# Low parts, complex differences and rotation products of the Hyena and attention layers: from GpSimd and VectorE in turn to VectorE alone

## The chip, the cores and the metric

The kernel runs on one core of one Trainium2 chip. The metric is the device time of one execution in microseconds (us); the median of several runs is compared. Engines are named as in the profile: PE is TensorE (PEld its weight load), DVE is VectorE, ACT is ScalarE, POOL is GpSimd, SP is SyncE, which issues nearly all loads.

## The reference, cut to what matters

Two stacks of two layers work on 256 tokens of width 1024. The first stack is untouched by the change. The second is a Hyena layer and an attention layer, each followed by a mixture of 16 experts:

```python
for i in range(DEPTH):
    u = rms_norm_2(h, mix_norm_g[i])
    if i % N_MIXERS == 0:
        proj = u @ hy_w_in[j]                       # 1024 x 2560
        main_in, cq = proj[..., :3 * D_MAIN], proj[..., 3 * D_MAIN:]
        main = hyena_mixer(main_in, hy_short_w[j], k_fft, hy_skip[j])
    else:
        proj = u @ at_w_in[j]                       # 1024 x 1536
        ...
        q = apply_axial_rope(rms_norm_2(q, at_q_norm_g[j]), cos, sin)
        kk = apply_axial_rope(rms_norm_2(kk, at_k_norm_g[j]), cos, sin)
        main = blocked_gqa(q, kk, vv)
    cross = memory_cross_attn(cq, mem_n, w_mem_kv[i])
    h = h + jnp.concatenate([main, cross], axis=-1) @ w_out[i]
    h = h + expert_choice_ffn(rms_norm_2(h, ffn_norm_g[i]), router_w[i], ...)
```

`hyena_mixer` is a short filter of three taps, then twice a long convolution by Fourier transform, `irfft(rfft(z) * k)`, and a gate.

## The kernel before, in words

Everything is float32. A product of two float32 matrices is made of three matmuls: each operand is split into a high part (a rounded copy) and a low part (what the rounding left out), and `mm3` (L303 to L305) adds high times high, high times low and low times high. `split` (L283) makes the parts of a weight tile: ACT writes the high part `hi` (L290), and then `next(lo_engines[0])` (L291), POOL and DVE in turn, writes the low part `lo` as a subtraction. In the output projection both parts lie in one tile `hl`. There are three `hi` and three `lo` buffers, so the fourth split waits until PE has used the first. A weight unit of the input projection is a 128x1024 tile, and 24 matmuls use it.

The Hyena layer (`hyena_layer`) computes the input projection as units of a pipeline (`dense_T`, tiles `psT`); `short` (L1324 to L1331) takes each result from PSUM, scales it by the row norm `nR` and applies the three taps into `uv` and `ux`, which PE then transposes (L1349). `nR` comes from a chain of small DVE instructions (L359, L360, L311 to L322, L365), a matmul by the identity (`psr`, L370) and a copy (L372). Four tasks `chain(o, n)`, for two orders and two halves of the channels, transform (`psz`), multiply by the filter in complex numbers (four products `ya`, L1368 to L1371, a difference, L1372, and a sum, L1373), split the result into `yh` and `yl` (L1376, L1377), transform back (`psy`), gate, and in the second order split the gated result into `ah` and `al` (L1397, L1398). `out_second` is the output projection (`psO`).

The attention layer (`attention_layer`) projects, scales (`qk_done`), and rotates (`rotate`): each query and key is multiplied by a cosine table (L1465) and its swapped halves by a sine table (L1463, into `rot`). Attention of pairs of heads follows (`attend`), with the softmax on DVE and ACT, and the same output projection.

Each of the two layers ends with the router (`route`) and the experts, whose weights (1.5 MB loads) stream through a ring of SBUF slots; a slot is loaded again when its last reader is done. Instructions of one engine run in the order of the program, which the framework's scheduler sets from the code; an instruction that waits holds all behind it on its engine. The engines on which low parts are made are in three lists:

```python
lo_engines = [cycle((G, V))]
LO1 = (G, V)
LO2 = (V, G, V)
LO3 = (G, V)
```

`LO1` holds from the start of the Hyena layer, `LO2` from that of the attention layer and `LO3` in its output projection.

Of the kernel before, what the change touches and what calls it, by code (L numbers as in the profile page):

```python
# [12 lines left out]
F32 = mybir.dt.float32  # L13
# [5 lines left out]
ALU = mybir.AluOpType  # L19
# [180 lines left out]
def build(ctx, tc, I, C, out, upto="all", dbg=None):  # L200
# [75 lines left out]
        S.activation(junk[:, :1], after, AF.Exp, scale=0.0)  # L276

    lo_engines = [cycle((G, V))]
    LO1 = (G, V)
    LO2 = (V, G, V)  # L280
    LO3 = (G, V)

    def split(src, shape, together=False):  # L283
        if together:
# [1021 lines left out]
    def hyena_layer(hy, ring, nm, c2, kd, kvd, state):  # L1306
        lo_engines[0] = cycle(LO1)
        state["go"] = True
        sw = c2["sw"]
        sk = cols[:, at["hy_skip_2"]:at["hy_skip_2"] + 12]  # L1310
        w_in = rows_of(I["hy_w_in_2"][0])
        u = {n: hy.tile([128, 6, T], F32, name=f"u{n}") for n in ("v", "x1", "x2")}
        cqT = hy.tile([128, 2, T], F32, name="cqT")
        kv = memory_load(hy, kvd)
        ready, box, busy = set(), {}, []
        has = lambda n, bs: (lambda: all((n, b) in ready for b in bs))

        def proj(n, c0, **kw):

            def short(b0, ps):  # L1320
                while nm.R is None:
                    pipe.tick()
                tmp = hy.tile([128, 2, T], F32, tag="tmp", name="tmp")
                V.tensor_tensor(tmp, ps, nm.R[:, None, :].to_broadcast([128, 2, T]), op=ALU.mult)  # L1324
                for q in range(2):
                    b = b0 + q
                    cb = c0 // 128 + b
                    o = u[n][:, b]
                    S.activation(o, tmp[:, q], AF.Copy, scale=sw[:, 18 + cb:19 + cb])
                    V.scalar_tensor_tensor(o[:, 1:], tmp[:, q, :T - 1], sw[:, cb:cb + 1], o[:, 1:], op0=ALU.mult, op1=ALU.add)  # L1330
                    V.scalar_tensor_tensor(o[:, :T - 1], tmp[:, q, 1:], sw[:, 36 + cb:37 + cb], o[:, :T - 1], op0=ALU.mult, op1=ALU.add)  # L1331
                    ready.add((n, b))

            return dense_T(ring, w_in[:, :, c0:c0 + 768], nm.xh, nm.xl, short, **kw)

        def chain(o, n):

            bs = range(3 * n, 3 * n + 3)
            c = slice(384 * n, 384 * n + 384)
            z = u["x1" if o else "v"]  # L1340
            yield from wait(has("z" if o else "v", bs))
            kf = hy.tile([128, 4, 384], F32, tag="uv" if o and n else "kf", name="kf")
            nc.sync.dma_start(kf, kd[2 * o + n])
            zz = hy.tile([128, 2, 2, 384], F32R, tag="z", name="zz")
            zh, zl = zz[:, 0], zz[:, 1]
            for par in range(2):
                ps = B("pst", [128, 384])
                for j in range(3):
                    PE.transpose(ps[:, 128 * j:128 * j + 128], z[:, 3 * n + j, par::2], ident)  # L1349
                S.activation(zh[:, par], ps, AF.Copy)  # L1350
                V.tensor_tensor(zl[:, par], ps, zh[:, par].bitcast(F32), op=ALU.subtract)
            yield from wait(lambda: "F" in box)
            Fh, Fl, Vh, Vl = box["F"]
            yield from wait(lambda: len(busy) < 1)
            busy.append((o, n))
            yh = hy.tile([128, 4, 384], F32R, tag="yh", name="yh")
            yl = hy.tile([128, 4, 384], F32R, tag="yl", name="yl")
            yield
            for f in range(2):
                pz = []  # L1360
                for part in range(2):
                    ps = B("psz", [128, 384])
                    fc = slice(part * 256 + f * 128, part * 256 + f * 128 + 128)
                    for t in range(2):
                        mm3(ps, Fh[:, t, fc], Fl[:, t, fc], zh[:, t], zl[:, t], t == 0, t == 1)
                    pz.append(ps)
                a = [hy.tile([128, 384], F32, tag="ya", name="ya") for _ in range(4)]
                V.tensor_tensor(a[0], pz[0], kf[:, f], op=ALU.mult)  # L1368
                V.tensor_tensor(a[1], pz[1], kf[:, 2 + f], op=ALU.mult)
                V.tensor_tensor(a[2], pz[0], kf[:, 2 + f], op=ALU.mult)  # L1370
                V.tensor_tensor(a[3], pz[1], kf[:, f], op=ALU.mult)  # L1371
                G.tensor_tensor(a[0], a[0], a[1], op=ALU.subtract)  # L1372
                V.tensor_tensor(a[2], a[2], a[3], op=ALU.add)  # L1373
                for part in range(2):
                    b = 2 * part + f
                    S.activation(yh[:, b], a[2 * part], AF.Copy)  # L1376
                    (G if part and not o else V).tensor_tensor(yl[:, b], a[2 * part], yh[:, b].bitcast(F32), op=ALU.subtract)  # L1377
                yield
            gate = u["x2" if o else "x1"]
            yield from wait(has("x2" if o else "x1", bs))  # L1380
            if o:
                yield from wait(lambda: "a" in box)
            yield
            for cb in range(3):
                b = 3 * n + cb
                i = 6 * o + b
                sz = hy.tile([128, T], F32, tag="sz", name="sz")
                S.activation(sz, z[:, b], AF.Copy, scale=sk[:, i:i + 1])
                ps = B("psy", [128, T])
                cc = slice(128 * cb, 128 * cb + 128)  # L1390
                for f in range(4):
                    mm3(ps, yh[:, f, cc], yl[:, f, cc], Vh[:, f], Vl[:, f], f == 0, f == 3)
                V.scalar_tensor_tensor(sz, ps, rn[:, i:i + 1], sz, op0=ALU.mult, op1=ALU.add)
                if o:
                    ah, al = box["a"]
                    V.tensor_tensor(sz, sz, gate[:, b], op=ALU.mult)
                    S.activation(ah[:, b], sz, AF.Copy)  # L1397
                    (V if n else G).tensor_tensor(al[:, b], sz, ah[:, b].bitcast(F32), op=ALU.subtract)  # L1398
                    ready.add(("a", b))
                else:  # L1400
                    V.tensor_tensor(gate[:, b], sz, gate[:, b], op=ALU.mult)
                    ready.add(("z", b))
                yield
            busy.remove((o, n))

        for o in range(2):
            for n in range(2):
                pipe.spawn(chain(o, n))
        pipe.feed(proj("v", 1536, need=lambda i: nm.halves > i, k_major=True))
        F = []  # L1410
        for name in ("fwd", "inv"):
            raw = ring.one(C[name])
            hi = hy.tile(list(raw.shape), F32R, name=name + "h")
            lo = hy.tile(list(raw.shape), F32R, name=name + "l")
            S.activation(hi, raw, AF.Copy)
            V.tensor_tensor(lo, raw, hi.bitcast(F32), op=ALU.subtract)
            F += [hi, lo]
        box["F"] = F
        pipe.feed(proj("x1", 0))
        wq = ring.one(w_in[:, :, 2304:2560])  # L1420

        def cq_done(j, ps):
            V.tensor_tensor(cqT, ps, nm.R[:, None, :].to_broadcast([128, 2, T]), op=ALU.mult)
            ready.add("cq")

        ct = pipe.spawn(cross_task(kv, cqT, hy, lambda: "cq" in ready, lambda: box.get("a"), (V, S)))
        pipe.feed(dense_T(ring, None, nm.xh, nm.xl, cq_done, tiles=[wq[:, 0:4], wq[:, 4:8]]))
        pipe.feed(proj("x2", 768))
        pipe.flush()
        box["a"] = ah, al = [xtp.tile([128, 8, T], F32R, tag=f"x{s}", name=f"a{s}") for s in "hl"]  # L1430
        pipe.feed(out_second(ring, I["w_out_2"][0], ah, al, state, lambda k: ct[1] if k > 5 else ("a", k) in ready))
        pipe.flush()

    def attention_layer(late, pool, ring, nm, c2, kvd, state, wqk):
# [17 lines left out]
        def rotate(i):  # L1452
# [7 lines left out]
            for t in range(2):  # L1460
                for j, a, nh in ((1, 768, 4), (0, 512, 4)) if i else ((0, 0, 8),):
                    for g in range(2):
                        G.tensor_tensor(hx(rot[:, t, a:a + 64 * nh])[:, :, :, g], hx(qk[:, t, a:a + 64 * nh])[:, :, :, 1 - g],  # L1463
                                        xhf(tg[:, j, t, 1])[:, None, :, g].to_broadcast([128, nh, 2, 16]), op=ALU.mult)
                    V.tensor_tensor(hv(qk[:, t, a:a + 64 * nh]), hv(qk[:, t, a:a + 64 * nh]), tg[:, j, t, 0][:, None, :].to_broadcast([128, nh, 64]), op=ALU.mult)  # L1465
            s2 = ss.rearrange("p t h -> p (t h)")
# [523 lines left out]
    o, ss = fin  # L1990
# [31 lines left out]
```

## Time and profile before

| what | value |
|---|---|
| median of 3 runs | 1913.12 us (1909.66 to 1913.76) |
| profiled execution | 1915.09 us, of which 1913.3 us are the span from the first to the last instruction |
| PE busy | 1643.7 us, 86% of the span |
| DVE busy | 981.1 us, 51% |
| ACT busy | 665.7 us, 35% |
| POOL busy | 540.2 us, 28%, 330 instructions |
| read from HBM | 483.41 MB |

The busy share is a mean over stages with different limits. Times below are from the start of the span: the Hyena layer lies at about 976 to 1127, the experts behind it end at 1450, the attention layer reaches to 1567, and the second experts run to the end.

### The profile page before, as it was taken

The numbers are of one execution on the slowest core, as the hardware profiler recorded it, in microseconds if no ns is written. First come the engines' busy times: TensorE is split into PE (matmuls) and PEld (weight loads), VectorE is DVE, ScalarE is ACT, GpSimd is POOL, SyncE is SP. The second block draws the span as 40 slices with busy tenths as digits, with TensorE's granted clock in tenths as the row PEclk, the third lists the DMA queues.
The fourth block names the chain that finished last, engine by engine and source line by source line (L and its number), as shares of the span: only waits on it lengthen the run. The fifth ranks groups of instructions, "written<-read, shape, count | busy, mean of one in ns | idle before, by whom it ended". The sixth has DMA issues, their size and how long they took to land. (4 is left out here: it accounts for less than half of the span.)

```text
span 1913.3 us, 27291 instructions
## 1 busy us (share of the span) xinstructions
PE 1643.7 (86%) x11139; PEld 1201.3 (63%) x11139; DVE 981.1 (51%) x1642; ACT 665.7 (35%) x1100; POOL 540.2 (28%) x330
## 2 busy tenths in 40 slices
PE   8899988999998999999989989676667999766665
PEld 7898977788988979899978765222224655211221
DVE  7987467666489865754568763010104873100102
ACT  4346444454443464545444432000003552000000
POOL 4532455754445325444434220000002220000001
PEclk9999999999999999999999989898988999898987
DMA  6443554455633435755443679999999768999997
GB/s 237 128 133 123 179 181 157 162 194 170 211 125 102 161 124 174 259 196 182 152 160 121 221 285 420 425 425 425 425 413 335 265 247 362 425 426 424 426 420 254
DMA packets 136516, 490.42 MB, mean 256 GB/s; under 512 B 11152, under 2 KB 32067, under 8 KB 115911
## 3 DMA queue, kind: packets, MB, share of 16 engines
q1 hardware_dynamic: 135919, 488.11, 67.8%
q8 instruction: 87, 1.43, 0.3%
q10 hardware_dynamic: 472, 0.57, 0.1%
q14 instruction: 38, 0.31, 0.0%
HBM read 483.41 MB, written 5.24 MB: 255 GB/s over the span
## 5 line engine op out<-in xcount | busy, mean ns | idle before, releaser
L291 POOL TENSOR_TENSOR lo<-w,hi 128x1024 fp32r<-128x1024 f32 (+3 forms) x163 | 379.1, 2327 | 806.5 <-ACT hi L290 776.4
L290 ACT ACTIVATE hi<-w 128x1024 fp32r<-128x1024 f32 (+3 forms) x330 | 327.3, 997 | 347.7 <-PE psT L305 178.9
L304 PE MATMUL psT<-xh,lo 128*128 128x256 f32 x1328 | 382.1, 288 | 12.4 <-POOL lo L291 12.4
L303 PE MATMUL psT<-xh,hi 128*128 128x256 f32 x1328 | 388.6, 293 | 2.0 <-ACT hi L290 2.0
L305 PE MATMUL psT<-xl,hi 128*128 128x256 f32 x1328 | 381.6, 287 | 0.0
L291 DVE TENSOR_TENSOR lo<-w,hi 128x1024 fp32r<-128x1024 f32 (+3 forms) x167 | 223.2, 1337 | 145.4 <-ACT hi L290 144.7
L304 PEld LDWEIGHTS psT<-xh,lo 128*128 128x128 f32 x1328 | 259.5, 195 | 18.1 <-POOL lo L291 14.2
L303 PEld LDWEIGHTS psT<-xh,hi 128*128 128x128 f32 x1328 | 259.2, 195 | 10.1 <-issue 5.9
L305 PEld LDWEIGHTS psT<-xl,hi 128*128 128x128 f32 x1328 | 259.3, 195 | 1.8 <-issue 1.8
L1738 PE MATMUL psx<-w,late 128*32 128x256 f32 (+1 forms) x1024 | 155.3, 539 | 75.8 <-DMA w<-in_exp_w_up 40.5
L1738 PEld LDWEIGHTS psx<-w,late 128*32 128x32 f32 x1024 | 47.0, 115 | 181.5 <-issue 74.2
L1738 PE MATMUL psx<-w,xg 128*32 128x256 f32 (+1 forms) x1024 | 124.1, 538 | 36.6 <-DMA w<-in_exp_w_up 19.9
L1790 PE MATMUL psy<-w,late 128*32 128x512 f32 x576 | 95.3, 596 | 38.2 <-DMA w<-in_exp_w_down 34.3
L1774 ACT ACTIVATE yy<-psy,rslot 128x512 fp32r<-128x512 f32 (+1 forms) x17 | 11.3, 662 | 320.7 <-PE psy L1790 249.7
L1738 PEld LDWEIGHTS psx<-w,xg 128*32 128x32 f32 x1024 | 39.9, 116 | 117.5 <-issue 60.6
L305 PE MATMUL acc<-lo,hh 128*128 128x512 f32 x256 | 100.7, 393 | 1.9 <-POOL lo L291 1.9
L304 PE MATMUL acc<-hi,hlo 128*128 128x512 f32 x256 | 100.8, 394 | 0.0
L303 PE MATMUL acc<-hi,hh 128*128 128x512 f32 x256 | 100.5, 393 | 0.0
L1982 POOL TENSOR_TENSOR o<-X,gf 128x256 f32<-128x256 f32 (+1 forms) x6 | 6.1, 1042 | 326.5 <-DVE X L1780 326.5
L1775 DVE SCALAR_TENSOR_TENSOR yy<-psy,rslot,yy 128x512 fp32r<-128x512 f32 (+1 forms) x17 | 12.2, 719 | 163.4 <-ACT yy L1774 162.9
L1754 DVE TENSOR_TENSOR late<-late,psx 128x512 f32<-128x512 f32 (+1 forms) x16 | 8.1, 550 | 166.8 <-PE psx L1738 166.8
L1790 PEld LDWEIGHTS psy<-w,late 128*32 128x32 f32 x576 | 26.6, 109 | 102.6 <-DMA w<-in_exp_w_down 52.4
(494 smaller groups left out, 2945.3 us busy)
## 6 DMA issues: line engine op xcount, KB each, us to landing
w<-in_exp_w_gate SPq DMA_DIRECT2D x64, 1536.0 KB, 27.8
w<-in_exp_w_up SPq DMA_DIRECT2D x64, 1536.0 KB, 29.5
w<-in_exp_w_down SPq DMA_DIRECT2D x48, 1536.0 KB, 28.5
w<-in_w_in SPq DMA_DIRECT2D x39, 1024.0 KB, 5.1
w<-in_w_up SPq DMA_DIRECT2D x32, 1024.0 KB, 5.7
w<-in_w_down SPq DMA_DIRECT2D x32, 1024.0 KB, 6.8
w<-in_exp_w_down SPq DMA_DIRECT2D x18, 1024.0 KB, 14.3
w<-in_w_out SPq DMA_DIRECT2D x10, 1024.0 KB, 5.6
```

The costliest lines, as they stand in the source:

```text
L290: S.activation(hi, src, AF.Copy)
L291: next(lo_engines[0]).tensor_tensor(lo, src, hi.bitcast(F32), op=ALU.subtract)
L303: PE.matmul(ps, lh, rh, start=start, stop=False)
L304: PE.matmul(ps, ll, rh, start=False, stop=False)
L305: PE.matmul(ps, lh, rl, start=False, stop=stop)
L1738: mm = PE.matmul(pg[nm][n][32 * e:32 * e + 32, :c1 - c0], xg[gr // 2][:, k, 128 * (gr % 2) + 32 * e:128 * (gr % 2) + 32 * e + 32], wt[e][: ...
L1754: V.tensor_tensor(hid[:, c], sg[:, :n], pg["up"][i][:, :n], op=ALU.mult)
L1774: S.activation(yh, py, AF.Copy, scale=rs[:, 2, gr:gr + 1])
L1775: V.scalar_tensor_tensor(yl, py, rs[:, 2, gr:gr + 1], yh.bitcast(F32), op0=ALU.mult, op1=ALU.subtract)
L1790: PE.matmul(py[n][32 * e:32 * e + 32], hT[:, k, 32 * e:32 * e + 32], wt[e][:, k - k0, 512 * n:512 * n + 512], start=k == 0, stop=k == 5, t ...
L1982: G.tensor_tensor(o[:, t, c], X[:, t, c], gf[:, c], op=ALU.mult)
```

## The change

All low parts of the two layers, the complex difference (L1372), all `yl` and `al`, and the sine products of the rotation are issued on DVE. POOL keeps the memsets, the small tables of the router and part of the router's row copies. The first stack keeps its two engines. The code:

```diff
     lo_engines = [cycle((G, V))]
-    LO1 = (G, V)
-    LO2 = (V, G, V)
-    LO3 = (G, V)
+    LO1 = LO2 = LO3 = (V,)
...
-                G.tensor_tensor(a[0], a[0], a[1], op=ALU.subtract)
+                V.tensor_tensor(a[0], a[0], a[1], op=ALU.subtract)
                 V.tensor_tensor(a[2], a[2], a[3], op=ALU.add)
                 for part in range(2):
                     b = 2 * part + f
                     S.activation(yh[:, b], a[2 * part], AF.Copy)
-                    (G if part and not o else V).tensor_tensor(yl[:, b], a[2 * part], yh[:, b].bitcast(F32), op=ALU.subtract)
+                    V.tensor_tensor(yl[:, b], a[2 * part], yh[:, b].bitcast(F32), op=ALU.subtract)
...
-                    (V if n else G).tensor_tensor(al[:, b], sz, ah[:, b].bitcast(F32), op=ALU.subtract)
+                    V.tensor_tensor(al[:, b], sz, ah[:, b].bitcast(F32), op=ALU.subtract)
...
-                        G.tensor_tensor(hx(rot[:, t, a:a + 64 * nh])[:, :, :, g], hx(qk[:, t, a:a + 64 * nh])[:, :, :, 1 - g],
+                        V.tensor_tensor(hx(rot[:, t, a:a + 64 * nh])[:, :, :, g], hx(qk[:, t, a:a + 64 * nh])[:, :, :, 1 - g],
                                         xhf(tg[:, j, t, 1])[:, None, :, g].to_broadcast([128, nh, 2, 16]), op=ALU.mult)
```

The scheduler sets a new order on each engine, and line numbers of the changed kernel are lower by two. The first place is DVE at the start of the Hyena layer, from the sum of squares (L354, L352 after the change) on. Here `lo` is the low part of a weight tile, `xl` that of the normalised input, `invl` that of the inverse transform's table, and `ms`, `nr`, `rh` and `rt` are the small tiles of the norm. Before:

```order
L354 SCALAR_TENSOR_TENSOR junk,ss<-X 128x512
L359 TENSOR_TENSOR ms<-ss 128x2
L360 TENSOR_SCALAR ms<-ms 128x2
L311 TENSOR_SCALAR nr<-ms 128x2
L312 TENSOR_SCALAR rh<-ms 128x2
L320 TENSOR_TENSOR rt<-rh,nr 128x2
L291 TENSOR_TENSOR lo<-w,hi 128x1024
L321 TENSOR_TENSOR rt<-rt,nr 128x2
L347 SCALAR_TENSOR_TENSOR xl<-pst,cols,xh 128x256 x2
L322 SCALAR_TENSOR_TENSOR nr<-rt,nr 128x2
```

The same place after the change:

```order
L352 SCALAR_TENSOR_TENSOR junk,ss<-X 128x512
L289 TENSOR_TENSOR lo<-w,hi 128x1024 x3
L345 SCALAR_TENSOR_TENSOR xl<-pst,cols,xh 128x256 x2
L357 TENSOR_TENSOR ms<-ss 128x2
L1414 TENSOR_TENSOR invl<-w,invh 128x1024
L345 SCALAR_TENSOR_TENSOR xl<-pst,cols,xh 128x256 x2
L358 TENSOR_SCALAR ms<-ms 128x2
L289 TENSOR_TENSOR lo<-w,hi 128x1024
L309 TENSOR_SCALAR nr<-ms 128x2
L310 TENSOR_SCALAR rh<-ms 128x2
L318 TENSOR_TENSOR rt<-rh,nr 128x2
L289 TENSOR_TENSOR lo<-w,hi 128x1024
```

Three low parts now stand ahead of the norm's first small instruction and two among the others, where one stood after the first five and one further down; on PE, the matmul `psr` that needs the norm's end stands behind 80 matmuls of the projection instead of 56.

The second place is DVE in the last Hyena chain, from the second pair of complex products on. `ya` are the products, their difference and their sum, `yl` the low parts, `hl` those of the output projection's weights, `sz` the gated result. Before:

```order
L1368 TENSOR_TENSOR ya<-psz,kf 128x384
L1369 TENSOR_TENSOR ya<-psz,kf 128x384
L1370 TENSOR_TENSOR ya<-psz,kf 128x384
L1371 TENSOR_TENSOR ya<-psz,kf 128x384
L1377 TENSOR_TENSOR yl<-ya,yh 128x384
L1373 TENSOR_TENSOR ya<-ya 128x384
L1377 TENSOR_TENSOR yl<-ya,yh 128x384
L1393 SCALAR_TENSOR_TENSOR sz<-psy,rn,sz 128x256 x2
```

After the change:

```order
L1366 TENSOR_TENSOR ya<-psz,kf 128x384
L1367 TENSOR_TENSOR ya<-psz,kf 128x384
L1368 TENSOR_TENSOR ya<-psz,kf 128x384
L1369 TENSOR_TENSOR ya<-psz,kf 128x384
L1370 TENSOR_TENSOR ya<-ya 128x384
L1371 TENSOR_TENSOR ya<-ya 128x384
L289 TENSOR_TENSOR hl<-w,hl 128x512
L1375 TENSOR_TENSOR yl<-ya,yh 128x384 x2
L289 TENSOR_TENSOR hl<-w,hl 128x512
L1391 SCALAR_TENSOR_TENSOR sz<-psy,rn,sz 128x256
```

The difference (L1370) has joined the queue ahead of the sum, and two low parts of weights stand around the two `yl`.

## Rows read from the trace of the kernel before

**Rows 1.** The page, part 4: the chain that ended last, by engine.

```profile
DMA 29%; PE 7%; DVE 3%; SPq 1%; issue 1%; ACT 1%; POOL 0%; ACTq 0%; DVEq 0%; POOLq 0%
```

**Rows 2.** The same chain in order of time: start, length, what.

```profile
1152.50 2.83 PE psx L1738 x32
1155.34 15.84 DMA w<-in_exp_w_down
...
1597.21 12.86 DMA w<-in_exp_w_down
```

**Rows 3.** Busy time by stretch: length, engines, PEclk, DMA share, GB/s.

```profile
1140.00:1145.00 5.00, 4.78 (x28) 2.71 (x32) 2.67 (x7) 1.58 (x3) 0.00 (x0) 0.50 0.03 12
...
1580.00:1585.00 5.00, 4.86 (x39) 1.77 (x37) 2.00 (x5) 1.58 (x3) 0.00 (x0) 0.66 0.16 29
```

**Rows 4.** POOL's groups, 955 to 1127: busy us, mean ns, idle before.

```profile
L291 POOL TENSOR_TENSOR lo<-w,hi 128x1024 fp32r<-128x1024 f32 x13 | 33.2, 2559 | 56.6 <-ACT hi L290 55.4 <-DVE ux L1331 1.1
L291 POOL TENSOR_TENSOR hl<-w,hl 128x512 fp32r<-128x512 f32 x8 | 10.9, 1366 | 22.2 <-ACT hl L290 14.8 <-DVE tmp L1324 6.2 <-issue 1.2
L1372 POOL TENSOR_TENSOR ya<-ya 128x384 f32<-128x384 f32 x8 | 8.1, 1011 | 19.6 <-DVE ya L1369 14.2 <-DVE sm L781 3.3 <-ACT hl L290 2.2
L1377 POOL TENSOR_TENSOR yl<-ya,yh 128x384 fp32r<-128x384 f32 x4 | 4.3, 1065 | 4.7 <-ACT yh L1376 4.7
L1398 POOL TENSOR_TENSOR al<-sz,ah 128x256 fp32r<-128x256 f32 x3 | 2.5, 830 | 4.2 <-ACT ah L1397 4.2
```

**Rows 5.** DVE's groups in the same stretch.

```profile
L291 DVE TENSOR_TENSOR lo<-w,hi 128x1024 fp32r<-128x1024 f32 x13 | 16.1, 1242 | 13.3 <-ACT hi L290 13.3
L1330 DVE SCALAR_TENSOR_TENSOR ux<-tmp,sw,ux 128x255 f32<-128x255 f32 x12 | 11.1, 953 | 2.7 <-ACT ux L1329 2.7
L1377 DVE TENSOR_TENSOR yl<-ya,yh 128x384 fp32r<-128x384 f32 x12 | 8.8, 731 | 3.8 <-ACT yh L1376 3.5
...
L291 DVE TENSOR_TENSOR hl<-w,hl 128x512 fp32r<-128x512 f32 x8 | 5.7, 718 | 6.5 <-ACT hl L290 6.5
...
L1331 DVE SCALAR_TENSOR_TENSOR ux<-tmp,sw,ux 128x255 f32<-128x255 f32 x12 | 5.4, 472 | 0.0
```

**Rows 6.** Timeline of POOL and DVE while the row norm is made.

```profile
975.72 4.95 POOL L291 TENSOR_TENSOR lo<-w,hi 128x1024 fp32r<-128x1024 f32 x2 [8.93 <-ACT hi L290]
...
976.15 2.19 DVE L359 TENSOR_TENSOR ms<-ss 128x2 f32<-128x2 f32 x1
978.37 2.32 DVE L360 TENSOR_SCALAR ms<-ms 128x2 f32<-128x2 f32 x1
...
987.04 2.19 DVE L322 SCALAR_TENSOR_TENSOR nr<-rt,nr 128x2 f32<-128x2 f32 x1
989.27 0.29 DVE L365 COPY nrb<-nr 128x256 f32<-128x256 f32 x1
```

**Rows 7.** What PE waited for, 955 to 1127: total us, times, longest.

```profile
PE pst L1349 <- DVE ux L1401: 3.0, 3, 1.5
PE psr L370 <- DVE nrb L365: 2.9, 1, 2.9
PE pst L1349 <- DVE uv L1331: 2.6, 2, 1.9
PE psy L303 <- ACT yh L1376: 2.1, 2, 1.4
PE pst L1204 <- DVE p L789: 1.6, 1, 1.6
```

**Rows 8.** Attention, 1455 to 1567: a POOL group and a DVE group.

```profile
L1463 POOL TENSOR_TENSOR rot<-qk,tg 128x128 f32<-128x128 f32 x8 | 4.8, 629 | 6.2 <-DVE qk L272 6.2
L1465 DVE TENSOR_TENSOR qk<-qk,tg 128x256 f32<-128x256 f32 x4 | 3.9, 1016 | 0.0
```

**Rows 9.** What PE waited for in the attention layer, 1470 to 1567.

```profile
PE psl L1194 <- DVE cqT L1543: 2.5, 1, 2.5
PE pst L1498 <- DVE qp L1490: 1.7, 2, 1.5
```

## The prediction, as it was put on record

> **What bounds the kernel now.** I began with the chain that ended last, by engine, because a kernel with PE busy for 86% of the span could be bound by PE or by its loads. DMA holds most of the listed shares of that chain [rows 1]. In order of time the chain has two stretches of back-to-back expert loads, from 1155 and from 1597, and each is entered from the first expert's matmuls (`psx`) [rows 2]. So the loads fix how long the experts last, and what happens before them fixes when they start. The second thing to see is whether the loads could start earlier. In the 5 us in which the first expert begins, the DMA engines are busy for 0.03 of the time, and 0.16 in the same stretch of the second layer [rows 3]: the ring of slots is full and waits for the experts to read it. A Hyena or attention layer that ends earlier therefore moves everything behind it. Nothing else of the change matters: what it saves inside the two layers counts in full, up to about 5 us a layer without help from earlier loads, and beyond that as far as slots come free earlier too.
>
> Inside the layers I read what PE waits for. In Hyena the five largest waits make 12.2 us, nearly all for results of DVE (`uv`, `ux`, the norm, a softmax) or of ACT behind DVE and POOL (`yh`) [rows 7]; in attention two waits for DVE make 4.2 us [rows 9]. Then I asked why DVE is late. Its groups show one form at two prices: L1331 and L1330 are the same operation on the same shape, directly one behind the other, yet L1331 takes 472 ns and L1330 953 ns [rows 5]. The timeline shows the reason most plainly in the norm: two instructions on two numbers a row take 2.19 and 2.32 us, from 976.15 to 980.69, exactly while POOL writes two low parts until 980.67, and L322 takes 2.19 us later, while the copy of 128x256 behind it needs 0.29 [rows 6]. DVE instructions that read SBUF stand still while POOL computes.
>
> The Trainium skill has this as a rule (SBUF — State Buffer, section "SBUF: two separate sides"): DVE and GpSimd share one pair of SBUF ports as an exclusive lock, and whichever comes second is blocked for the whole instruction, if it has two SBUF inputs against a GpSimd instruction that reads SBUF, or uses a two-port mode. The trace agrees (2.32 us at L360). By this rule every such stall goes in both layers, since POOL is left with memsets and router tables, and the first rival below loses weight; by the rows alone only the groups named are known to stall.
>
> **What the change removes.** POOL loses 10 of the 13 low parts of 128x1024 (the first three are the MLP's), 8 of 128x512, 8 differences, 4 `yl` and 3 `al`, at 2.56, 1.37, 1.01, 1.07 and 0.83 us [rows 4], and attention's low parts and rotations.
>
> **What it adds to DVE.** In Hyena: 10 x 1.24 = 12.4 us and 8 x 0.72 = 5.7 us. For 128x384 no undisturbed row of DVE stands here; between 0.47 us (128x255) and 0.72 us (128x512) I take 0.60 by size, so 12 x 0.60 = 7.2 us; three `al` at no more than 0.47 each, 1.4 us. Together 26.7 us [rows 5].
>
> **What DVE gets back.** L1330: 12 x (0.953 - 0.472) = 5.8 us. The norm: 2.19 + 2.32 + 2.19 less three times at most 0.29, that is 5.8 us. `yl`: 12 x (0.73 - 0.60) = 1.6 us. That is 13.2 us from these groups alone [rows 5, 6], so DVE does at most 13.5 us more in some 150 us.
>
> **What that is worth on the path.** I take four terms, each between nothing and the whole wait of PE, in places where added work could also make it worse.
>
> T1, the start of Hyena. After the change DVE has, between the sum of squares and `nrb`, five low parts and `invl` (6 x 1.24 = 7.4 us), four `xl` at about 0.47 (1.9 us) and eleven small instructions at no more than 0.29 (3.2 us): at most 12.5 us after 976.1, so 988.6 instead of 989.27 [rows 5, 6]. PE now has 24 matmuls more to do before it needs the result. I take the whole wait of 2.9 us. For `uv`, each wait has two L1330 ahead of it, 2 x 0.48 us each, so 1.9 of 2.6 us. T1 is -5 us, between 0 and -5.5 [rows 7].
>
> T2, the middle. The three waits for `ux` (3.0 us) have the same two stalls ahead, 2.9 us, but low parts of 1.24 us now stand in that queue: half, 1.5 us. The softmax wait of 1.6 us: 1.0. T2 is -2.5 us, between +0.8 (a low part of 1.24 us in front of each of the three, less the 2.9 us of stalls) and -4.6 [rows 5, 7].
>
> T3, the last chains. The difference falls from 1.01 to 0.60 us and ACT's `yh` waits for it, so 0.4 us in each pair, and 12 matmuls of the output projection now stand ahead of the last `psy`, work for PE while it waits. Of 2.1 us I take 1.5, between 0 and 2.1 [rows 4, 7].
>
> T4, attention. Ahead of `cqT`, four L1465 lose 4 x (1.02 - 0.47) = 2.2 us of stall, and eight rotations and one low part join. A rotation of 128x128 costs on DVE between 0.29 and 0.47 us, taken as 0.38: 3.0 + 1.2 - 2.2 = +2.0 us [rows 5, 6, 8]. Against that, low parts that POOL made in 2.4 to 2.6 us are there a microsecond earlier each, and so PE's projection ahead of it; I count this place as nothing. Before `qp` stalls go and four rotations come: 1.0 of 1.7 us. T4 is -1 us, between +2 and -4.2 [rows 9].
>
> The Trainium skill (VectorE: DVE Perf Modes, section "The TRN2 errata — SBUF-src ops pay a fixed extra latency per instruction") gives (N+151)/0.96 ns for float32 tensor_tensor, an estimate of 0.29 us for N = 128. By it the eight rotations cost 2.3 us instead of 3.0 and the place of `cqT` would be +1.3 instead of +2.0; no row shows it for this shape.
>
> The sum is -10 us. SP's order moves one load of the up projection ahead of gate loads; rows 3 show the loads done before the experts start, so I cost it at nothing; without that cover it is one load, some 2 us if the eight behind 1155 share their 15.84 us evenly [rows 2, 3]. The profiled execution took 1915.09 us, 1913.3 of them span, so it would be 1905 us; it lies 2.0 us over the median of the runs, 1913.12, so the median should be 1903 us.
>
> **Rivals.** (a) The queue gives it back: DVE does 13.5 us more, and only T1, where PE has other work, comes through, less 3 us of new waits in the middle: -2 us, 1911. For it speaks that DVE also holds the softmax and the evacuations. Against it speaks the doubled price of L1330 [rows 5].
>
> (b) Slower: a low part at the head of DVE's queue waits. POOL could sit idle before its low parts at no cost, 56.6 us before 13 [rows 4]; DVE sat 13.3 us before its 13, 1.0 us each [rows 5]. If the 10 moved ones and the 8 `hl` wait in DVE's queue, everything behind them waits too. At 1.0 us each on ten of them the gain is gone; at 1.6 us it is +6 us, 1919. The place is the projection, 976 to 1060, where three buffers are all there is. Against it: the new order places them where their inputs should be ready.
>
> (c) The loads don't follow: the Hyena layer ends 9 us earlier but slots come free no earlier, so only about 5 us of idle loading are gained [rows 3], with T4: -6 us, 1907.
>
> (d) All listed waits vanish: 12.2 + 4.2 = 16.4 us, 1897, and waits too small to list could go as well.
>
> **How the numbers follow.** Forecast (1898 to 1908, most likely 1903) 0.58, (a) 0.15, (b) 0.12, (c) 0.08, (d) 0.07. The range 1892 to 1912 leaves out (b) and the upper part of (a). The bound of 0.2%, what a measurement of this kernel can tell from no change, is 3.8 us. Forecast, (c), (d) and a little of (a) are faster: 0.75; the rest of (a) is the same: 0.13; (b) is slower: 0.12.
>
> **What would show it.** Right: L359, L360 and L322 of the norm at about 0.2 us, L1330 as short as L1331, the wait of `psr` under 1 us, and the two first stretches of expert loads entered some 9 and 10 us earlier. POOL should keep about 32 low parts and products less in Hyena and 25 less in attention. Wrong: if DVE's idle time before low parts grows by more than 10 us, (b) holds; if the loads have no idle time left before the experts, (c) does. The prediction fails as a whole if the stalls were DVE's own and stay without POOL.

## The result, and the profile after

The changed kernel takes 1887.35 us (median of 6 runs, 1885.52 to 1896.32) against 1912.95 us for the kernel before (6 runs, 1909.66 to 1913.76); the ratio is 0.9874, 95% interval 0.9853 to 0.9894. It is faster by 25.6 us, where the prediction had 10 and a range that ended at 1892. The profiled execution took 1887.0 us, 1885.2 of them span. In the changed kernel the lines from `split` on are two lower than before.

The chain that ended last, by engine (page, part 4), answers to [rows 1]:

```profile
DMA 28%; PE 26%; DVE 2%; ACT 1%; SPq 1%; issue 1%; POOL 0%; ACTq 0%; DVEq 0%
```

The same chain in order of time, [rows 2]:

```profile
1129.17 2.83 PE psx L1736 x32
1132.02 16.60 DMA w<-in_exp_w_down
...
1601.89 26.98 DMA w<-in_exp_w_gate
```

The first stretch of loads is entered 23.3 us earlier (1132.02 against 1155.34). The second is entered 4.7 us later, so the forecast's 10 us can't be looked for there: the experts of that layer begin 25.7 us earlier (first `psx` at 1555.35 against 1581.03), and the chain goes through their matmuls until then. Between the two traces the last sum of X in the attention layer comes 27.1 us earlier and the last instruction 28.1 us. Stretches of 5 us in which the first expert of each layer begins, [rows 3]:

```profile
1118.80:1123.80 5.00, 4.14 (x43) 2.07 (x42) 3.12 (x7) 1.59 (x3) 0.00 (x0) 1.00 0.06 20
...
1554.00:1559.00 5.00, 4.85 (x30) 2.02 (x33) 1.74 (x4) 1.58 (x3) 0.00 (x0) 0.53 0.00 0
```

The ring is full again at both places: the loads wait for the experts, which now begin 21.2 and 25.7 us earlier. DVE while the norm is made, [rows 6]:

```profile
978.82 0.15 DVE L357 TENSOR_TENSOR ms<-ss 128x2 f32<-128x2 f32 x1
...
980.88 0.16 DVE L358 TENSOR_SCALAR ms<-ms 128x2 f32<-128x2 f32 x1
...
985.38 0.16 DVE L320 SCALAR_TENSOR_TENSOR nr<-rt,nr 128x2 f32<-128x2 f32 x1
985.58 0.29 DVE L363 COPY nrb<-nr 128x256 f32<-128x256 f32 x1
```

The instructions of 2.19, 2.32 and 2.19 us are 0.15 to 0.16 us now. DVE's groups, 955 to 1142, [rows 5]:

```profile
L289 DVE TENSOR_TENSOR lo<-w,hi 128x1024 fp32r<-128x1024 f32 x23 | 27.9, 1221 | 8.9 <-ACT hi L288 8.9
L1329 DVE SCALAR_TENSOR_TENSOR ux<-tmp,sw,ux 128x255 f32<-128x255 f32 x12 | 5.3, 483 | 0.0
L1328 DVE SCALAR_TENSOR_TENSOR ux<-tmp,sw,ux 128x255 f32<-128x255 f32 x12 | 5.3, 482 | 0.7 <-ACT ux L1327 0.7
```

L1328 (L1330 before) costs half of what it did and as much as its neighbour. The 953 ns before were a mean of two prices: six of the 12 took 0.47 us and six 1.0 to 2.3. Each of the six began while POOL computed and ended 0.28 us after the end of POOL's instruction. One of them in the kernel before, with the instruction of POOL:

```profile
1079.26 1.33 POOL L291 TENSOR_TENSOR hl<-w,hl 128x512 fp32r<-128x512 f32 x1 [8.95 <-ACT hl L290]
```

```profile
1079.61 1.26 DVE L1330 SCALAR_TENSOR_TENSOR ux<-tmp,sw,ux 128x255 f32<-128x255 f32 x1 [0.17 <-ACT ux L1329]
```

DVE also waits less for its 23 low parts (8.9 us) than it did for 13 (13.3). What PE waited for, 955 to 1105, [rows 7]:

```profile
PE pst L341 <- DVE X L989: 0.6, 1, 0.6
PE psy L301 <- ACT yh L1374: 0.5, 1, 0.5
PE psy L302 <- DVE yl L1375: 0.4, 1, 0.4
PE psr L368 <- DVE nrb L363: 0.3, 1, 0.3
PE psT L302 <- DVE lo L289: 0.3, 1, 0.3
PE psT L301 <- ACT hi L288: 0.2, 1, 0.2
```

These are all: 2.3 us. Before, all such waits from 955 to 1126 made 16.1 us, 12.2 of them the five of [rows 7]. The largest of the others, at 977 in the kernel before:

```profile
PE psT L304 <- POOL lo L291: 1.3, 1, 1.3
```

And in the attention layer, 1436 to 1545, [rows 9]:

```profile
PE pst L1202 <- ACT p L778: 1.0, 1, 1.0
...
PE psl L1192 <- ACT p L778: 0.6, 1, 0.6
...
PE pst L1202 <- DVE p L787: 0.3, 1, 0.3
```

Both waits of [rows 9] are gone, and 1.9 us of new ones, for the softmax, have come.

The waits are not all of it. The busy times by stretch (columns as in [rows 3]; behind POOL's stands the granted clock as a share of 2.4 GHz) of the kernel before, first the layer up to its last sum of X, then 980 to 985, 990 to 995 and 1055 to 1060:

```profile
955.00:1126.00 171.00, 154.89 (x987) 139.13 (x986) 126.73 (x213) 76.96 (x143) 59.17 (x42) 0.97 0.52 183
...
980.00:985.00 5.00, 5.00 (x33) 5.00 (x33) 4.86 (x13) 1.82 (x3) 0.67 (x1) 0.72 0.30 60
...
990.00:995.00 5.00, 5.00 (x32) 5.00 (x32) 0.58 (x2) 1.06 (x1) 0.00 (x0) 0.70 0.64 211
...
1055.00:1060.00 5.00, 3.16 (x12) 1.89 (x13) 5.00 (x11) 2.74 (x8) 1.73 (x2) 0.79 0.47 144
```

The first three of them in the kernel after:

```profile
955.00:1104.60 149.60, 147.15 (x979) 133.26 (x979) 123.08 (x243) 76.77 (x142) 7.16 (x8) 1.00 0.58 209
...
980.00:985.00 5.00, 5.00 (x44) 5.00 (x43) 4.42 (x15) 1.85 (x4) 0.00 (x0) 1.00 1.01 382
...
990.00:995.00 5.00, 4.86 (x40) 4.69 (x40) 5.00 (x10) 3.03 (x6) 0.00 (x0) 1.00 0.57 226
```

PE is busy throughout 980 to 985 in both kernels, but with 33 matmuls before and 44 after: for part of that stretch the granted clock lay on its lower level (1.2 GHz) before, and on its upper level (2.4 GHz) throughout after. It fell three times in the layer of the kernel before: after PE's waits of 1.3 us at 977, of 2.9 us (`psr`) at 987 and of 1.6 us (`p`) at 1055. It did not fall after waits of 1.9 us (`uv`) at 999, 1.5 us (`ux`) at 1039 and 1.4 us (`yh`) at 1111. The clock's shortfall (what its share lacks of 1, times the length) adds up to 5.1 us from 955 to 1126 before, and to nothing from 955 to 1105 after. DVE is busy for less in the layer (123.08 against 126.73 us), although it has some 30 instructions more (x243 against x213).

### The profile page after: what moved, and what is told of

It is laid out like the page before. It is cut to its first block, busy times and chain, and to the rows that moved or that the text cites. A ratio compares the mean times of both kernels' runs of the same rounds, so it can differ in the third digit from the quotient of the medians.

```text
span 1885.2 us, 27267 instructions
## 1 busy us (share of the span) xinstructions
PE 1640.0 (87%) x11139; PEld 1200.5 (64%) x11139; DVE 980.2 (52%) x1700; ACT 666.3 (35%) x1100; POOL 460.4 (24%) x272
## 4 chain that ended last, share of the span: by engine, by line
DMA 28%; PE 26%; DVE 2%; ACT 1%; SPq 1%; issue 1%; POOL 0%; ACTq 0%; DVEq 0%
DMA w<-in_exp_w_up 9%; DMA w<-in_exp_w_gate 9%; DMA w<-in_exp_w_down 9%; PE psT L301 3%; PE psT L302 3%; PE psT L303 3%; PE psx L1736 2%; PE acc L301 2%; PE acc L302 2%; PE acc L303 2%; PE psl L1192 1%; SPq L187 1%; PE psM L301 1%; PE psM L302 1%; PE psM L303 1%; PE psO L301 1%
## 5 line engine op out<-in xcount | busy, mean ns | idle before, releaser
L289 POOL TENSOR_TENSOR lo<-w,hi 128x1024 fp32r<-128x1024 f32 (+3 forms) x148 | 343.4, 2321 | 420.5 <-ACT hi L288 391.4
L289 DVE TENSOR_TENSOR lo<-w,hi 128x1024 fp32r<-128x1024 f32 (+3 forms) x182 | 237.6, 1307 | 138.6 <-ACT hi L288 138.3
L1736 PE MATMUL psx<-w,late 128*32 128x256 f32 (+1 forms) x1024 | 159.7, 571 | 74.5 <-DMA w<-in_exp_w_up 41.6
L1773 DVE SCALAR_TENSOR_TENSOR yy<-psy,rslot,yy 128x512 fp32r<-128x512 f32 (+1 forms) x17 | 12.2, 720 | 158.7 <-ACT yy L1772 158.2
L1751 DVE SCALAR_TENSOR_TENSOR late<-psx,rslot,late 128x512 f32<-128x512 f32 (+1 forms) x16 | 9.1, 613 | 157.1 <-ACT late L1750 157.1
```

Source lines behind the costliest of these rows:

```text
L289: next(lo_engines[0]).tensor_tensor(lo, src, hi.bitcast(F32), op=ALU.subtract)
L1736: mm = PE.matmul(pg[nm][n][32 * e:32 * e + 32, :c1 - c0], xg[gr // 2][:, k, 128 * (gr % 2) + 32 * e:128 * (gr % 2) + 32 * e + 32], wt[e][: ...
L1751: V.scalar_tensor_tensor(sg[:, :n], pg["gate"][i][:, :n], r2, sg[:, :n], op0=ALU.mult, op1=ALU.mult)
L1773: V.scalar_tensor_tensor(yl, py, rs[:, 2, gr:gr + 1], yh.bitcast(F32), op0=ALU.mult, op1=ALU.subtract)
```

## The experiments

Theory A: DVE's instructions on SBUF operands stand still while POOL reads SBUF, and the gain is the end of that. Theory B: no standing still matters; POOL's instructions were merely twice as long, and what needs their results comes earlier now. Theory C: the gain is the new order of the instructions. Further rivals stand in the expectations. In the table the Hyena layer's length goes from the start of the last sum of X in the MLP (L991 before) to that of the last in the layer (L1249), and attention's from `psr` to its last sum of X, in the profiled execution of each; the lengths are sharper than the medians, since the experts' stretches can differ by 2 to 3 us between kernels that are equal there. The kernel before had medians of 1912.16 to 1912.95 us beside these runs.

| kernel | median, us | ratio to before (95%) | Hyena layer, us | attention, us |
|---|---|---|---|---|
| before | 1912.95 | | 151.1 | 88.9 |
| after | 1887.35 | 0.9853 to 0.9894 | 131.3 | 83.2 |
| low parts only | 1890.07 | 0.9872 to 0.9897 | 134.3 | 83.2 |
| all but low parts | 1914.10 | 0.9998 to 1.0017 | 152.4 | 86.4 |
| after, POOL reads | 1908.52 | 0.9972 to 0.9990 | 150.0 | 83.3 |
| after, POOL's memsets | 1893.30 | 0.9882 to 0.9910 | 131.3 | 83.2 |
| Hyena layer only | 1893.57 | 0.9888 to 0.9918 | 131.3 | 88.9 |
| first three low parts | 1904.07 | 0.9948 to 0.9975 | 141.7 | 88.9 |
| after, POOL reads a table | 1907.90 | 0.9969 to 0.9986 | 150.7 | 83.2 |
| after, POOL reads one input | 1895.54 | 0.9899 to 0.9926 | 137.7 | 83.1 |
| all low parts of the first stack | 1840.87 | 0.9617 to 0.9649 | | |
| two of three there | 1864.95 | 0.9748 to 0.9775 | | |
| all arithmetic there | 1831.02 | 0.9562 to 0.9588 | | |

**Low parts only, and all but low parts.** The change in two halves.

```diff
-    LO1 = (G, V)
-    LO2 = (V, G, V)
-    LO3 = (G, V)
+    LO1 = LO2 = LO3 = (V,)
```

> The kernel before with only its three lists of low parts on DVE; differences, yl, al and rotations stay on POOL. Theory A (POOL's reading of SBUF holds DVE up, and the gain is the end of that): low parts are 36.5 of POOL's 51.4 us in the Hyena layer (10 x 2.56 + 8 x 1.37 against 8.1 + 4.3 + 2.5), so about 0.7 of the 25.6 us: 1895 us, between 1891 and 1899; the ux taps at under 0.6 us instead of 0.95. Theory B (no holding up; POOL's instructions were merely long, and what waits for their results comes earlier now): PE hardly waited for low parts, so at most a third: 1904 or more.

The other half is the kernel after with these three lists as before.

> The kernel after with the three lists of low parts as before (POOL in turn with DVE); differences, yl, al and rotations on DVE. Theory A: about 0.3 of the gain: 1905 us, between 1901 and 1909, ux taps still near 0.9 us. Theory B: the chains that PE waits for hold these instructions, so at least half of the gain: 1900 or less.

The first half gives 22.8 us, more than either theory had, though A's range is missed by only 1 us; the second gives nothing that can be measured, where A had some 8 us and B at least half of the gain. So A's way of sharing the gain out by POOL's busy time is wrong as well. The taps into `ux` in the second run, whose PE waits 4.7 us for `ux` instead of 3.0:

```profile
L1330 DVE SCALAR_TENSOR_TENSOR ux<-tmp,sw,ux 128x255 f32<-128x255 f32 x12 | 8.4, 733 | 1.7 <-ACT ux L1329 1.7
L1331 DVE SCALAR_TENSOR_TENSOR ux<-tmp,sw,ux 128x255 f32<-128x255 f32 x12 | 7.4, 652 | 0.0
```

Three first taps and one second are held there, of 1.0 to 2.6 us, each behind a low part that stays on POOL; in the kernel before it was six first taps and no second. The differences, `yl`, `al` and rotations are worth something only behind the low parts: the Hyena layer is 3.0 us shorter with them than without (131.3 against 134.3), but 1.3 us longer where the low parts stay on POOL (152.4 against 151.1). B falls with the two halves: it had at most a third for the first and at least half for the second.

**POOL reads for nobody.** Two kernels with the order of the kernel after, row by row, on PE, DVE, ACT and SP; only POOL has more to do, at the places where it made a low part of the Hyena layer: `turn` is 1 and 0 in turn there and 0 elsewhere, `parts` are the 128x256 pieces of `src` and `hi`, and `g` is the scratch tile. The first adds the subtractions, the second a small copy and memsets at the same place.

```diff
         next(lo_engines[0]).tensor_tensor(lo, src, hi.bitcast(F32), op=ALU.subtract)
+        if next(turn[0]):
...
+            for s1, h1 in parts:
+                G.tensor_tensor(g, s1, h1.bitcast(F32), op=ALU.subtract)
```

> The kernel after, with the order of PE, DVE, ACT and SP the same row by row, and one thing more: wherever POOL made a low part in the Hyena layer before, it now makes the same subtraction from the same two inputs in pieces of 128x256 into a scratch tile that nobody reads. Theory A: DVE is held up again in the Hyena layer: the norm's two small instructions at 2 us, ux taps near 0.9 us, and 10 to 16 us of the gain lost: 1897 to 1903. Theory B: nobody waits for the scratch tile, so within 2 us of the kernel after: 1885 to 1890, and ux taps at 0.47 us. Theory C (the gain is the new order of the instructions on PE, DVE and ACT): also 1885 to 1890.

```diff
+        if next(turn[0]):
...
+            G.tensor_copy(g[:, :2], parts[0][1][:, :2].bitcast(F32))
+            for _ in parts + parts:
+                G.memset(g, 0.0)
```

> The same as the run with POOL's reading, but POOL only writes: at each of these places a copy of two columns, to set the moment, and then twice as many memsets of 128x256 into the scratch tile. Theories A, B and C: within 2 us of the kernel after, 1885 to 1890, and ux taps at 0.47 us. If POOL at work in any way holds DVE up (theory A'), it stands where the run with POOL's reading stands, 1897 or more, less what the shorter busy time of POOL takes off.

With the reading, 21.2 of the 25.6 us are gone again, more than the 10 to 16 that A had, and the layer is 18.7 us longer than in the kernel after. Its groups, 955 to 1142, first the larger of POOL's two on `ghost` (40 of 56 pieces; all 56 take 58.2 us), then DVE:

```profile
L295 POOL TENSOR_TENSOR ghost<-w,hi 128x256 f32<-128x256 f32 x40 | 42.8, 1071 | 49.1 <-ACT hi L289 25.8 <-issue 20.9
```

```profile
L1335 DVE SCALAR_TENSOR_TENSOR ux<-tmp,sw,ux 128x255 f32<-128x255 f32 x12 | 8.7, 761 | 0.0
L1378 DVE TENSOR_TENSOR ya<-ya 128x384 f32<-128x384 f32 x8 | 7.1, 887 | 0.0
...
L1329 DVE TENSOR_TENSOR tmp<-psT,nR 128x512 f32<-128x512 f32 x9 | 6.1, 682 | 4.6 <-PE psT L309 4.5
```

No instruction reads `ghost`; the only wait for it outside POOL is one of 2.1 us of ACT, for a high part's buffer that POOL still reads. And yet the first taps into `ux` (L1335) take 0.76 us instead of 0.48 and the sum of two SBUF tiles (`ya`) 0.89 instead of 0.55. The norm's two small instructions, for which A had 2 us, take 0.15 us as in the kernel after: they fell between POOL's pieces, and `invl` beside them takes 1.77 us instead of 1.22. What reads PSUM beside one SBUF tile (`tmp`) takes 0.68 us, as in the kernel after (0.69): it isn't held. With memsets, POOL and the first taps:

```profile
L296 POOL MEMSET ghost<- 128x256 f32 x112 | 35.4, 316 | 6.5
```

```profile
L1336 DVE SCALAR_TENSOR_TENSOR ux<-tmp,sw,ux 128x255 f32<-128x255 f32 x12 | 5.2, 477 | 0.6 <-ACT ux L1335 0.6
```

35.4 us of POOL that only writes leave DVE and the layer's length as they were. The same holds for the whole kernel: DVE's 1700 instructions, in the same order, are busy for 980.2 us in the kernel after, 1002.7 with the reading and 980.3 with the memsets. The median is 6 us above the kernel after, which no theory had; in the traces, where 4.7 us are between the two, the layers are equal and the whole of it lies in the two stretches of experts (2.4 us each). Whether that is more than scatter stays open. A and B part here, and C falls with the first of the two kernels, which has the new order and 4.4 us of the 25.6.

The Trainium skill (SBUF — State Buffer, section "SBUF: two separate sides") says that a DVE instruction with two SBUF inputs excludes a GpSimd instruction only where that one reads SBUF. The three rows of DVE beside POOL's reading and the row beside the memsets agree.

**A table, and one input.** POOL might have held the three `hi` buffers for longer with its reading. So it reads parts of a constant table (`tg`) instead, after a copy of two columns that sets the moment, and in a second kernel copies only.

```diff
+        if next(turn[0]):
...
+            G.tensor_copy(g[:, :2], parts[0][1][:, :2].bitcast(F32))
...
+            for _ in parts:
+                G.tensor_tensor(g, tab[:, :256], tab[:, 256:], op=ALU.subtract)
```

> The kernel after, and POOL with a copy of two columns at the old places, then as many subtractions of 128x256 as the run with POOL's reading has, but of two parts of a constant table, so that no weight tile, high part or buffer is held by POOL. Theory A (reading itself): where the run with POOL's reading stands, 1903 to 1912, with ux taps at 0.7 us. If that run lost its time because POOL held the high parts' three buffers longer (rival E): 1886 to 1894.

```diff
-            for _ in parts:
-                G.tensor_tensor(g, tab[:, :256], tab[:, 256:], op=ALU.subtract)
+            for _ in parts + parts:
+                G.tensor_copy(g, tab[:, :256])
```

> As the run with the table, with twice as many copies of 128x256 (one input) in place of the subtractions. If any reading of SBUF by POOL holds DVE's two-input instructions up, in proportion to its busy time: slower than the kernel after by 8 to 20 us, 1895 to 1907. If it takes two inputs on POOL's side: 1886 to 1894, and ux taps at 0.47 us.

The table costs what the reading of weights did (1907.90), so rival E falls: the reading counts, not what is held by it. DVE is busy for 1000.1 us with the table and 989.9 with the copies (980.2 in the kernel after). Single instructions show the same: of the 36 taps into `ux` and `uv`, 8 took over 0.52 us in the kernel before, 17 with POOL's reading, 18 with the table, 31 with the copies, and none in the kernel after or with the memsets. Every one of the long ones began while POOL was reading and ended 0.28 us after that instruction of POOL; beside the memsets 22 taps began and were not held. Copies of one input cost 8.2 us, with `ux` at 0.60 us: they hold DVE up too, less per microsecond (65.1 us of copies against 54.5 us of subtractions that cost 20.6 us). In the same groups of each kernel, the table's taps and then the copies':

```profile
L1338 DVE SCALAR_TENSOR_TENSOR ux<-tmp,sw,ux 128x255 f32<-128x255 f32 x12 | 8.9, 779 | 0.2 <-ACT ux L1337 0.2
```

```profile
L1338 DVE SCALAR_TENSOR_TENSOR ux<-tmp,sw,ux 128x255 f32<-128x255 f32 x12 | 6.8, 602 | 0.0
```

**The terms apart.** The kernel before with T1's low parts alone, and the kernel after without the attention layer's part.

```diff
-        lo_engines[0] = cycle(LO1)
+        lo_engines[0] = (V if k < 6 or k % 2 else G for k in range(999))
```

> The kernel before, with the first six low parts of the Hyena layer on DVE: three are taken from POOL, those beside the norm (975 to 990), nothing else. If what is gained at the start of the layer (term T1) is carried to the end, and the norm's stalls are most of it: 5 us by the forecast's term, 7.7 us by the place where the run of low parts alone has its first transposes: 1905 to 1908. If every reading of POOL costs about alike, three of 18 low parts are worth 3 to 4 us: 1909. If the queue gives it back (rival (a)): 1911 or more.

```diff
-    LO1 = LO2 = LO3 = (V,)
+    LO1 = (V,)
+    LO2 = (V, G, V)
+    LO3 = (G, V)
...
-                        V.tensor_tensor(hx(rot[:, t, a:a + 64 * nh])[:, :, :, g], hx(qk[:, t, a:a + 64 * nh])[:, :, :, 1 - g],
+                        G.tensor_tensor(hx(rot[:, t, a:a + 64 * nh])[:, :, :, g], hx(qk[:, t, a:a + 64 * nh])[:, :, :, 1 - g],
```

> The kernel after with the attention layer as before: its low parts on POOL in turn with DVE, its rotation products on POOL. By the two traces the attention layer came 5.9 us nearer to the start of its experts (its last sums of X are 27.1 us earlier, the first expert of the layer ahead of it 21.2 us): so 1893 us, between 1891 and 1895. By the forecast's term T4, -1 us, it would be 1888.

Three instructions of POOL, 7.3 us of it, are worth 8.65 us at the end (1912.72 less 1904.07), a little over the first of the three expectations. In that kernel PE, from 980 to 990:

```profile
980.00:985.00 5.00, 5.00 (x44) 5.00 (x43) 4.46 (x14) 1.85 (x4) 0.00 (x0) 1.00 1.02 372
985.00:990.00 5.00, 4.71 (x40) 4.51 (x39) 3.06 (x8) 2.20 (x3) 0.18 (x1) 1.00 0.79 227
```

The clock stays at its upper level: 44 matmuls instead of 33. What PE still waits for there, 955 to 1115, and what it hardly waits for any more:

```profile
PE pst L1349 <- DVE uv L1331: 2.6, 2, 2.0
PE psy L303 <- ACT yh L1376: 2.1, 2, 1.4
PE pst L1204 <- DVE p L789: 0.8, 1, 0.8
...
PE psr L370 <- DVE nrb L365: 0.3, 1, 0.3
PE psT L304 <- DVE lo L291: 0.3, 1, 0.3
```

Attention's part is worth 6.2 us (1893.57 less 1887.35), as the traces had it. What PE waited for in attention in the kernel without it, 1440 to 1552:

```profile
PE psl L1194 <- DVE cqT L1543: 2.5, 1, 2.5
PE pst L1498 <- DVE qp L1490: 1.7, 2, 1.4
PE psT L304 <- POOL lo L291: 1.3, 1, 1.3
```

**The first stack.** If A holds, the layers that the change left alone lose time in the same way: 148 low parts of theirs are on POOL after the change. Three kernels, each the kernel after and:

```diff
-    lo_engines = [cycle((G, V))]
+    lo_engines = [cycle((V,))]
```

> The kernel after, and the low parts of the first stack on DVE alone too: 148 of POOL less. Theory A, carried over: PE is idle for some 47 us before 955, and in the Hyena layer two thirds of such idle time went with POOL's reading (21.3 to 6.9 us); here POOL keeps 100 us of other arithmetic, so a third to a half: 15 to 25 us faster than the kernel after, 1862 to 1872. Rival D (DVE becomes the bound): it is busy for 663 of the first 965 us, and 148 x 1.2 us come to that, 841 of 965, and in the first 120 us for 106 already: low parts are late there and the time rises: 1890 or more.

with `cycle((V, V, G))` at the same place:

> The kernel after, with two of three low parts of the first stack on DVE instead of one of two: some 50 low parts of POOL less. Theory A: a third of what the run with all of them on DVE gains, 5 to 8 us: 1879 to 1882. Rival D: DVE has about 60 us more to do there, so between no change and 5 us slower.

and with `(V,)` and the first stack's other `G.tensor_tensor` on V:

> As the run with all low parts of the first stack on DVE, and the rest of POOL's two-input arithmetic of the first stack on DVE too (products of the scan, rotations, sums of the gates, the filters' sums and low parts; about 100 us of POOL). Theory A: 3 to 8 us faster than with the low parts alone. Rival D: DVE at 841 of 965 us gets some 50 us more, so slower than with the low parts alone by as much as 10 us.

They take 1840.87, 1864.95 and 1831.02 us. Against the kernel after that is 46.5 us where 15 to 25 were expected, 22.4 where 5 to 8 were, and for the last 9.9 us beyond the first where 3 to 8 were; the last is 56.3 us under the kernel after and 81 under the kernel before. The first lines of the profile's pages for the first and the last of them:

```profile
PE 1616.7 (88%) x11139; PEld 1187.0 (65%) x11139; DVE 1004.9 (55%) x1848; ACT 669.8 (36%) x1102; POOL 129.3 (7%) x124
```

```profile
PE 1617.2 (89%) x11139; PEld 1187.0 (65%) x11139; DVE 1002.5 (55%) x1912; ACT 669.3 (37%) x1102; POOL 28.8 (2%) x60
```

Rival D is wrong because it priced what DVE gets and not what it gets back: 148 low parts of 1.22 us and less, some 170 us, raised its busy time by 24.7 us (980.2 to 1004.9). The two causes aren't parted here: before 955, PE in the kernel after still waits 13.4 us for low parts of POOL and 24.2 us for DVE, both of which shrink, and there is no run in which POOL reads for nobody in the first stack.

## Why the prediction was wrong

The direction and the mechanism were right. The chain was read rightly: the loads followed in full, and rival (c) is out. That DVE's instructions are held up by POOL's reading is shown by the runs with `ghost`. One sentence was too wide: not every DVE instruction that reads SBUF stands still (`tmp`, with its other input in PSUM, doesn't), and not whenever POOL computes (memsets hold nothing). Rival (a) is out (no new waits in the middle of Hyena), and (b) too: DVE's idle time before low parts fell by 4.4 us and did not grow by 10. `psr`, L1328 and the norm came out as foreseen. The rotation of 128x128 takes 0.29 us on DVE, not the 0.38 that I took. That is the estimate worked out from the Trainium skill's formula (VectorE: DVE Perf Modes, section "The TRN2 errata — SBUF-src ops pay a fixed extra latency per instruction").

What failed is the step "I take four terms, each between nothing and the whole wait of PE". The gain of a place was put at part of its listed wait and bounded by it; the clock behind a wait and the waits too small to list were put at nothing, without a reason. In Hyena the three terms came to 9 us, and the layer became 19.8 us shorter (151.1 to 131.3). Of the listed waits 11.4 us went where 8.8 were taken, of the others 2.4, and 5.1 us of the clock's shortfall: 18.9 together. By terms:

- T1, -5 and at most -5.5, was 2.9 us for `psr` and 1.9 for `uv`. The run with three low parts gives 8.65 us although `uv` is waited for as before (2.6 us). The wait of `psr` went (2.9 to 0.3 us), but so did the wait for a low part of POOL at 977 (1.3 to 0.3 us), which the five largest did not show, and the clock's shortfall behind the two, 3.4 us from 975 to 995, which I did not price at all. Later in that layer the wait for `p` fell by 0.8 us, and the clock did not fall behind it (1.7 us).
- T2 and T3, together -4: the Hyena layer alone gives 18.6 us (1912.16 less 1893.57), less that run's 8.65 about 10, `uv` among it. T3 was right: of the 2.1 us for `yh` 1.6 went, where I took 1.5. I took half of the `ux` waits because low parts join that queue; in fact all went. DVE got back not 13.2 us but some 28: 25.6 us of work joined it (10 x 1.22, 8 x 0.69, 12 x 0.55, 3 x 0.42) and it was busy for 3.7 us less, about 1 of that because the MLP ended 1.4 us earlier. The groups that I named were fewer than half of the stalls.
- T4, -1: measured -6.2. I counted `cqT` at nothing, since low parts and rotations join the queue in front of it. But the 2.5 us went, as did `qp` and, ahead of them, 1.3 us for a low part, against 1.9 us of new waits; and the clock's shortfall of 1.7 us behind `cqT` (rows below) went with them.

Attention in the kernel before, 1485 to 1495; in the kernel after the clock stays at 1.00 from 1440 to 1545:

```profile
1485.00:1490.00 5.00, 2.47 (x6) 1.00 (x5) 4.32 (x12) 0.02 (x1) 0.81 (x1) 0.80 0.62 213
1490.00:1495.00 5.00, 5.00 (x21) 3.55 (x19) 4.45 (x15) 1.97 (x5) 0.00 (x0) 0.86 0.27 111
```

Rival (d), 1897, was nearest and still 10 us short: it had all listed waits, 16.4 us, and neither the others nor the clock. The two layers became 19.8 and 5.7 us shorter, 25.5 together, and the medians differ by 25.6. The agreement is closer than the method: the waits and the clock named here explain 18.9 and 4.3 of the two lengths, between the two traces lie 28.1 us, of which 1.4 had been gained before the Hyena layer, and the experts' stretches differ by 2 to 3 us by themselves. The parts are read from one trace each, and how far the clock's part alone would go was not tried in a run of its own; the three low parts of T1 show it beside the waits, not apart from them.

## What to carry to other kernels

Where one form of a VectorE instruction on SBUF operands shows two prices, look at what GpSimd reads at that time: 55 us of GpSimd subtractions whose result nobody read cost 21 us here, and 35 us of memsets cost VectorE nothing. Before calling VectorE too full for the work, subtract the stalls that go with it: 148 more subtractions made it busy for 25 us more, and the kernel 46 us faster. And price a stretch of TensorE from all its waits, not from the largest, and look behind each wait whether the clock fell: here it did behind three waits of the Hyena layer, which cost 5.1 us more, and not behind three others of 1.4 to 1.9 us.

## What had not been expected

Two things beside the clock. One-input copies on GpSimd hold VectorE too, but at some 0.13 us of kernel time for each microsecond against 0.38 for subtractions. And the holding goes both ways. POOL's subtractions of 128x256 for nobody took between 0.72 and 1.82 us, 17 of the 56 over half as long again as the shortest. Of these 17, 16 began while DVE was making a low part and ended 0.6 us after it. Of the 112 memsets of that size 109 lay within a tenth of their shortest, 0.31 us.
